# First two w_mod pieces on four column tiles, sums of x first, six accumulators by turns, modulation batches moved ahead of their units

## Chip, cores and metric

One core of one Trainium2 chip runs the whole program in one launch. The metric is the device time of that launch in microseconds. TensorE is called PE here, VectorE DVE, ScalarE ACT, GpSimd POOL, and SyncE, whose queue issues nearly all loads, SP.

## What is computed

A single layer of a decoder trunk for 256 prompt tokens and 8 sample tokens, which share the weights: 264 columns in all, kept feature-major as 16 blocks of 128 features. Cut to what matters here:

```python
mod = jax.nn.silu(c) @ prm['w_mod'] + prm['b_mod']
shift, scale, gate = jnp.split(mod[:, None, :], 3, axis=-1)
h = rmsnorm(x, prm['g_pre']) * (1 + scale) + shift
(u_a, v_a, z_a, x_b, z_b, q, k, v, q_i, k_i, w_i, z_c, g_m) = split_proj(h @ prm['w_in'])
# three branches (spatial gating, RG-LRU, indexed attention), gated, merged
o = merged @ prm['w_out']
x = x + gate * rmsnorm(o, prm['g_post'])
```

The matrix `w_mod` (2048 by 6144) is multiplied with 9 conditioning vectors only (1 prompt, 8 samples). Nothing that uses `h` can start before shift and scale of at least one block of 128 features are there, and every such block needs its columns of `w_mod` over all 2048 rows.

## The kernel before, in words

All matrix products with 264 columns are done in three fp32r products of split operands: the weight as high part `wh` and rest `wl`, the other side as `hh` and `hl` (`wh*hh + wh*hl + wl*hh`). ACT makes `wh` by a copy (L313), DVE makes `wl` by a subtraction (L317), in halves of 512 columns.

**Pieces of w_mod.** The 16 blocks of `h` are made in six pieces (`PIECES`, L48): block 0, block 1, blocks 2 and 3, 4 to 7, 8 to 11, 12 to 15. A piece's columns of `w_mod` come in loads of 512 KB (4, 4, 8, 16, 16, 16 of them). Here m3.5 is load 5 of piece 3. `mod_item` (L417) holds loads back until `BATCH` of them (1, 2, 2, 4, 4, 4) are there, and then multiplies them (`mod_products`, L405): the stationary side is the conditioning, padded to 32 columns, so that an output takes 32 partitions, and up to four groups of columns of a load go to four column tiles of the array. In pieces 0 and 1 there are two groups of 128 columns, in piece 2 four of 128, in pieces 3 to 5 four of 256. After a piece's last batch `mod_piece` (L467) copies the sums, turns them (`mod_turn`, L446) and makes `hh` and `hl` of its blocks, one step after each product of the units that follow.

**Units.** The weights of the products with 264 columns come in loads of 512 KB, called units here: unit 0 to unit 63 belong to the first 32 output tiles (`EARLY`), which are computed piece by piece of `h`: units 0, 1, 2, 3, 5, 7 of the kernel before hold one block for 8 tiles, units 4 and 6 two blocks for 4 tiles, units 8 to 15 blocks 2 and 3 for 4 tiles each, units 16 to 31 blocks 4 to 7 for 2 tiles each, and so on. Each unit has 24 matmuls, whatever its shape. A tile's partial sum is copied out of PSUM after its first piece (L1042: DVE for even tiles, ACT for odd) and added to by DVE after each further one (L1044). All later products accumulate all 16 blocks in PSUM.

**The order of the work** is the list `STREAM` (L82): `FOLLOW` (L51) says which units go with a piece, and the loop over `units` puts the loads of the next piece between them, spread evenly by `MOD_BY`. Each engine does its instructions in the order of this list. `next_load` (L259) issues loads on SP in the list's order as buffers come free: 6 for units (`raw0` to `raw5`), 8 for w_mod (`rawm0` to `rawm3` and four in `rawx`). A unit's buffer is free when its `wl` is made, a w_mod buffer when PE has multiplied it and the next unit has begun. SP takes its loads strictly in order.

**Accumulators.** PSUM has 8 banks: 3 in the ring `acc`, 3 in the ring `s`, 2 in the ring `t`. Products of the early tiles take `acc`, and every fourth takes `s`, which the turned modulation (`modT`) and the norm's rows (`rsP`, `rbP`) use too.

**The start.** SP loads the conditioning, x in four parts, two loads of piece 0, the first parameters `par`, the other two loads, then units and piece 1. PE runs 40 products of ones first (L186). `norm_x` (L375) sums the squares of x; its first step (the sums, and a product `rsP` on PE) is called after the first load of piece 0 has been multiplied (L1056), the second (`rbP`) after the fourth.

Of the kernel before, what the change touches and what calls it, by code (L numbers as in the profile page):

```python
# [15 lines left out]
P = 128  # L16
# [4 lines left out]
T = NP + NS  # L21
# [25 lines left out]
EARLY = 32  # L47
# [1 line left out]


FOLLOW = [[(0, 0, 1), (8, 0, 1), (16, 0, 1)],  # L51
          [(0, 1, 1), (24, 0, 2), (8, 1, 1), (28, 0, 2), (16, 1, 1)]]
FOLLOW += [[(j, k0, nk) for j in range(0, EARLY, 8 // nk)] for k0, nk in PIECES[2:]]
GATES = [(0, 8), (8, 8)]


NRAW = 6
AHEAD = 2
NEAR = 60
CUT = 2  # L60
MOD_BY = 22

BATCH = [1, 2, 2, 4, 4, 4, 4, 4]

# [14 lines left out]
MODS = _mods()  # L79


def _stream():  # L82


    items, n = [("m", 0, i) for i in range(len(MODS[0]))], 0
    for q, units in enumerate(FOLLOW):
        ms = [("m", q + 1, i) for i in range(len(MODS[q + 1]))] if q + 1 < len(PIECES) else []
        done = 0
        for x, (j, k0, nk) in enumerate(units):
            while done < len(ms) and (x == 2 if q == 0 else done * MOD_BY * len(units) <= x * EARLY * len(ms)):  # L90
                items.append(ms[done])
                done += 1
            items.append(("w", n, [(t, k0, nk) for t in range(j, j + 8 // nk)]))
            n += 1
        assert done == len(ms)
    gate = [("m", q, i) for q in range(len(PIECES), len(MODS)) for i in range(len(MODS[q]))]
    units = 0
    for j in range(EARLY, len(ORDER)):
        for k0 in (0, 8):
            items.append(("w", n, [(j, k0, 8)]))  # L100
            n += 1
            if gate and ORDER[j][0] in ("u", "za", "g0", "pa"):
                if units % 16 in (2, 4, 6, 8):
                    items.append(gate.pop(0))
                units += 1
    assert not gate
    return items
# [33 lines left out]
def trunk_kernel(ctx: ExitStack, tc: tile.TileContext, a: dict, o: dict):  # L141
    nc = tc.nc
    act, dve, pool, pe, sp = nc.scalar, nc.vector, nc.gpsimd, nc.tensor, nc.sync
# [15 lines left out]
    def acc(name):  # L159
        return ps.tile([P, 512], F32, name=name, tag="acc", bufs=3)  # L160

    def pss(name):
        return ps.tile([P, 512], F32, name=name, tag="s", bufs=3)
# [4 lines left out]
    copy = lambda out, x, scale=1.0: act.activation(out, x, AF.Copy, scale=scale)  # L168
# [20 lines left out]
    ident = const.tile([P, P], F32, name="ident")  # L189
# [54 lines left out]
    m0 = len(MODS[0])  # L244
# [10 lines left out]
    resting, units = [], [0]  # L255
# [103 lines left out]
        sp.dma_start(xr[:, 4 * i:4 * i + 4, :], a["xT"][:, 4 * i:4 * i + 4, :])  # L359
    while (i := next_load(0)) is not None:  # L360
        load(i)
        if i == 1:
            sp.dma_start(par[:, 0:C_SH], a["par"][:, 0:C_SH])
    sp.dma_start(par[:, C_SH:C_END], a["par"][:, C_SH:C_END])
    sp.dma_start(pti, bass.AP(tensor=a["pt"].tensor, offset=0, ap=[[0, P], [1, 16]]))
# [9 lines left out]
    def norm_x():  # L375
        add(sqacc, sums[0], sums[1])
        rows = rstd_rows([sqacc])
        next(rows)
        yield
        S["r"] = next(rows)  # L380
        yield
        copy(sqacc, S["r"])
        S["r"] = sqacc

    norm = norm_x()
    pool.tensor_copy(xs, xr[:, :, NP:T])
    dve.tensor_scalar(bsc1, prm(C_BMOD, KB, KB), 1.0, None, op0=OP.add)
    dve.tensor_scalar(hb, prm(C_BA, 0, 2 * KB), 0.5, None, op0=OP.mult)
# [6 lines left out]
    MOD = {}  # L395
# [1 line left out]
    done_h = set()  # L397


    def groups_of(q):  # L400
        width = MODS[q][0][0]
        groups = min(4, width // P)
        return groups, width // groups

    def mod_products(q, m, r):  # L405
        width, ks, _ = MODS[q][m]
        groups, n = groups_of(q)
        if m == 0:
            MOD[q] = pst("pmod")
        for x, k in enumerate(ks):  # L410
            for g in range(groups):
                c = x * width + g * n
                pe.matmul(MOD[q][32 * g:32 * g + 32, 0:n], cpad[:, k, :], r[:, c:c + n],  # L413
                          start=k == 0, stop=k == KB - 1, skip_group_check=True)


    def mod_item(i):  # L417
# [7 lines left out]
        if m == len(MODS[q]) - 1:  # L425
# [17 lines left out]
            else:  # L443
                tasks.spawn(mod_gate(q - len(PIECES)), 1)

    def mod_turn(q, ms):  # L446
        groups, n = groups_of(q)
        r = 32 * groups
        pt = pss("modT")
        for b in range(n // P):  # L450
            pe.transpose(pt[:, b * P:b * P + r], ms[0:r, b * P:(b + 1) * P], ident[0:r, 0:r])
        return pt[:, 0:n].rearrange("p (b g r) -> p b g r", b=n // P, g=4)

    def mod_rows(q):
        groups, n = groups_of(q)
        ms = w("ms")
        copy(ms[0:32 * groups, 0:n], MOD.pop(q)[0:32 * groups, 0:n])
        return ms

    def by_k(x, g):  # L460
# [6 lines left out]
    def mod_piece(q):  # L467
        k0, nk = PIECES[q]
        ms = mod_rows(q)
        yield 1  # L470
        pt = mod_turn(q, ms)
        ks = slice(k0, k0 + nk)
        g = groups_of(q)[0] // 2
        add(by_k(mB[:, ks, :], g), pt[:, :, 0:g, 0:9], by_k1(prm(C_BMOD, k0, nk), g))
        add(by_k(mA[:, ks, :], g), pt[:, :, g:2 * g, 0:9], by_k1(bsc1[:, ks], g))
        mul(mA[:, ks, :], mA[:, ks, :], prm(C_GPRE, k0, nk)[:, :, None].to_broadcast([P, nk, 9]))
        r = S["r"]
        ts, samples = {}, w("hsm")[:, 0:nk * NS].rearrange("p (k b) -> p k b", k=nk)
        for k in range(k0, k0 + nk + 1):
            if k < k0 + nk:  # L480
                t = ts[k] = w("h_")
                stt(t[:, 0:NP], xr[:, k, 0:NP], mA[:, k, 0:1], r[:, 0:NP], OP.mult, OP.mult)
                act.activation(hh[:, k, 0:NP], t[:, 0:NP], AF.Identity, bias=mB[:, k, 0:1])
                if k == k0:
                    mul(samples, xr[:, ks, NP:T], mA[:, ks, 1:9])
                    mul(samples, samples, r[:, None, NP:T].to_broadcast([P, nk, NS]))
                    add(samples, samples, mB[:, ks, 1:9])
                    copy(hh[:, ks, NP:T], samples)
            if k > k0:
                stt(hl[:, k - 1, 0:NP], ts[k - 1][:, 0:NP], mB[:, k - 1, 0:1], f32(hh[:, k - 1, 0:NP]), OP.add,  # L490
                    OP.subtract)
                if k == k0 + 1:
                    sub(hl[:, ks, NP:T], samples, f32(hh[:, ks, NP:T]))
                done_h.add(k - 1)
            yield 1
# [524 lines left out]
    ACC = {}  # L1020

    def product(j, k0, nk, wh, wl):
        kind, f = ORDER[j]
        if k0 == 0 and (kind, f) in BEFORE:
            BEFORE[kind, f]()
        early = j < EARLY
        last = k0 + nk == KB
        if early or k0 == 0:
            ACC[j] = pss("acc") if early and not last and j % 4 == 3 else acc("acc")
        c = ACC[j]  # L1030
        xh, xl = {None: (hh, hl), "a": (S.get("ah"), S.get("al")), "m": (S.get("mh"), S.get("ml"))}[RHS.get(kind)]
        assert RHS.get(kind) or done_h.issuperset(range(k0, k0 + nk))
        for kk in range(nk):
            k = k0 + kk
            for n, (x, y) in enumerate(((wh, xh), (wh, xl), (wl, xh))):
                pe.matmul(c[:, 0:T], x[:, kk * P:(kk + 1) * P], y[:, k, :],  # L1036
                          start=n == 0 and (kk == 0 if early else k == 0),
                          stop=n == 2 and (kk == nk - 1 if early else k == KB - 1))
        if early:
            pj = part[j // KB][:, j % KB, :]  # L1040
            if k0 == 0:
                (copy if j % 2 else dve.tensor_copy)(pj, c[:, 0:T])  # L1042
            elif not last:
                add(pj, c[:, 0:T], pj)  # L1044
            else:
                x = w("sum")
                add(x, c[:, 0:T], pj)
                tasks.spawn(POST[kind](f, x), 1)
        elif last:
            tasks.spawn(POST[kind](f, c[:, 0:T]), 1)  # L1050
        tasks.run()

    for i, it in enumerate(items):
        while (x := next_load(units[0])) is not None:
            load(x)
        if i == 1:  # L1056
            next(norm)
        late = it[0] == 'w' and ORDER[it[2][0][0]][0] == "zb"
        pieces = len(it[2]) if it[0] == "w" else 0
        if i >= m0 and not late:  # L1060
            split_plan()
            split_some(CUT // 2 if pieces > 2 else None)
        if it[0] == "m":
            mod_item(i)
            continue
        units[0] += 1
        wh, wl = SPLIT.pop(i)
        col = 0
        for j, k0, nk in it[2]:
            product(j, k0, nk, wh[:, col:col + nk * P], wl[:, col:col + nk * P])  # L1070
            col += nk * P
            if col == 4 * P:
                split_some()
        if late:
            split_plan(AHEAD - 1)
            split_some()
# [16 lines left out]
    p = pss("rsP")  # L1093
# [120 lines left out]
```

## Time and profile before

| | |
|---|---|
| median of 3 runs | 1578.3 us (1578.22 to 1578.94) |
| the profiled execution: its own time | 1578.65 us |
| its span on the core | 1577.0 us |
| PE busy | 1555.5 us (99%), 13353 matmul records |
| DVE busy | 982.5 us (62%) |
| ACT busy | 806.8 us (51%) |
| DMA | 326.26 MB, mean 207 GB/s |

A view lists times in microseconds from the span's start. "Idle before, releaser" is how long the engine stood idle just before an instruction, and whose instruction ended the wait. The helpers copy, mul, add, sub and stt stand under their own lines (L168 to L172). A matmul with fp32 operands shows as two records. PE's records overlap, since a matmul is pipelined: its pace is read from the distance of the starts, not from the durations. PEclk is the clock that PE was granted, 1.00 for 2.4 GHz and 0.50 for 1.2 GHz. For a DMA the profile gives the start of its issue on SP and the time from there until the data had landed.

### The profile page before, as it was taken

Reading aid. Unit: us, or ns where it says so; the run is one execution under the profiler, and the core shown is the slowest. Engines: PE = TensorE matmul, PEld = TensorE weight load, DVE = VectorE, ACT = ScalarE, POOL = GpSimd, SP = SyncE. Lnnn points to the kernel's source line nnn. Section 1 sums busy time; section 2 is a strip of 40 time slices with the busy share of each in tenths; the row PEclk is TensorE's granted clock in tenths of the full one; section 3 lists DMA queues with packets and bytes.
Section 4 is the critical chain, followed back from the end, with each engine's and each line's share of the span. In section 5 each row is a group of like instructions: output and inputs, shape, how many; then the busy total and the mean of one; then the engine's idle time right before and its main releaser. Section 6 shows DMA issues by size and latency. Waiting matters only on the chain.

```text
span 1577.0 us, 33367 instructions
## 1 busy us (share of the span) xinstructions
PE 1555.5 (99%) x13353; PEld 1516.0 (96%) x13353; DVE 982.5 (62%) x2097; ACT 806.8 (51%) x1628; POOL 133.7 (8%) x240
## 2 busy tenths in 40 slices
PE   8999999999999999999999999999999999999997
PEld 8789898999999999999999999999999999999997
DVE  6777589755567446455556544445777777766554
ACT  5334368555555444444444443344777777744442
POOL 0000027000000001000000000001221111100011
PEclk9999999999999999999999999999999999999999
DMA  9898863646555556556656676665555555555652
GB/s 376 333 353 305 310 199 121 229 160 206 169 176 174 189 185 201 182 180 216 224 190 202 224 277 223 205 205 168 168 173 168 188 180 174 177 183 183 240 177 81
DMA packets 94907, 326.26 MB, mean 207 GB/s; under 512 B 10784, under 2 KB 14240, under 8 KB 94368
## 3 DMA queue, kind: packets, MB, share of 16 engines
q1 hardware_dynamic: 93952, 322.98, 59.7%
q8 instruction: 105, 1.72, 0.4%
q10 hardware_dynamic: 800, 1.15, 0.2%
q14 instruction: 50, 0.41, 0.1%
HBM read 320.35 MB, written 3.67 MB: 205 GB/s over the span
## 4 chain that ended last, share of the span: by engine, by line
PE 83%; DVE 1%; POOL 0%; ACT 0%; issue 0%; DVEq 0%; POOLq 0%; ACTq 0%
PE acc L1036 78%; PE pmod L413 1%; PE spP L864 0%; PE sP L699 0%; PE oP L711 0%; PE giP L905 0%; PE gaP L905 0%; POOL qq L589 0%; PE ssP L748 0%; PE soP L772 0%; PE sP L698 0%; PE pT L706 0%; PE oP L713 0%; PE vaP L665 0%; DVE x L172 0%
## 5 line engine op out<-in xcount | busy, mean ns | idle before, releaser
L171 DVE TENSOR_TENSOR wl<-raw,wh 128x512 fp32r<-128x512 f32 x964 | 636.3, 704 | 368.3 <-ACT wh L168 358.8
L1036 PE MATMUL acc<-hh,wh 128*128 128x264 f32 x2832 | 816.7, 288 | 7.3 <-DVE part L170 3.9
L1036 PE MATMUL acc<-hl,wh 128*128 128x264 f32 x2832 | 804.1, 284 | 0.0
L1036 PE MATMUL acc<-hh,wl 128*128 128x264 f32 x2832 | 802.7, 283 | 1.4 <-DVE wl L171 1.3
L168 ACT ACTIVATE wh<-raw 128x512 fp32r<-128x512 f32 x964 | 551.8, 622 | 487.2 <-PE acc L1036 363.2
L1036 PEld LDWEIGHTS acc<-hh,wh 128*128 128x128 f32 x2832 | 534.1, 189 | 21.7 <-issue 13.0
L1036 PEld LDWEIGHTS acc<-hl,wh 128*128 128x128 f32 x2832 | 534.5, 189 | 0.8 <-DVE hl L171 0.2
L1036 PEld LDWEIGHTS acc<-hh,wl 128*128 128x128 f32 x2832 | 531.8, 188 | 1.9 <-DVE wl L171 1.9
L1036 PE MATMUL acc<-ah,wh 128*128 128x264 f32 x768 | 217.9, 284 | 0.0
L1036 PE MATMUL acc<-al,wh 128*128 128x264 f32 x768 | 217.6, 283 | 0.0
L1036 PE MATMUL acc<-ah,wl 128*128 128x264 f32 x768 | 217.4, 283 | 0.0
L1036 PEld LDWEIGHTS acc<-al,wh 128*128 128x128 f32 x768 | 144.7, 188 | 0.0
L1036 PEld LDWEIGHTS acc<-ah,wh 128*128 128x128 f32 x768 | 144.6, 188 | 0.0
L1036 PEld LDWEIGHTS acc<-ah,wl 128*128 128x128 f32 x768 | 144.0, 187 | 0.0
L170 DVE TENSOR_TENSOR part<-acc,part 128x264 f32<-128x264 f32 x120 | 48.7, 428 | 38.9 <-PE acc L1036 38.7
L1036 PE MATMUL acc<-mh,wh 128*128 128x264 f32 x256 | 72.6, 284 | 0.0
L1036 PE MATMUL acc<-ml,wh 128*128 128x264 f32 x256 | 72.5, 283 | 0.0
L1036 PE MATMUL acc<-mh,wl 128*128 128x264 f32 x256 | 72.5, 283 | 0.0
L836 POOL TENSOR_TENSOR mg<-mg,gp 128x264 f32<-128x264 f32 x16 | 12.0, 753 | 465.2 <-DVE gp L172 465.2
L1036 PEld LDWEIGHTS acc<-ml,wh 128*128 128x128 f32 x256 | 48.2, 188 | 0.0
L1036 PEld LDWEIGHTS acc<-mh,wh 128*128 128x128 f32 x256 | 48.2, 188 | 0.0
L1036 PEld LDWEIGHTS acc<-mh,wl 128*128 128x128 f32 x256 | 48.0, 187 | 0.0
(375 smaller groups left out, 1075.5 us busy)
## 6 DMA issues: line engine op xcount, KB each, us to landing
raw<-in_wall SPq DMA_DIRECT2D x482, 512.0 KB, 3.6
rawm<-in_wmod SPq DMA_DIRECT2D x64, 512.0 KB, 7.2
rawx<-in_wmod SPq DMA_DIRECT2D x32, 512.0 KB, 8.9
gkv<-in_ckv SPq DMA_DIRECT2D x32, 256.0 KB, 4.5
xr<-in_xT SPq DMA_DIRECT2D x4, 528.0 KB, 5.3
wrg<-in_wrg SPq DMA_DIRECT2D x1, 2048.0 KB, 12.8
x<-in_xp SPq DMA_DIRECT2D x1, 2048.0 KB, 8.1
out_yp<-x SPq DMA_DIRECT2D x8, 256.0 KB, 3.1
```

The costliest lines, as they stand in the source:

```text
L168: copy = lambda out, x, scale=1.0: act.activation(out, x, AF.Copy, scale=scale)
L170: add = lambda out, x, y: dve.tensor_tensor(out, x, y, OP.add)
L171: sub = lambda out, x, y: dve.tensor_tensor(out, x, y, OP.subtract)
L413: pe.matmul(MOD[q][32 * g:32 * g + 32, 0:n], cpad[:, k, :], r[:, c:c + n], start=k == 0, stop=k == KB - 1, skip_group_check=True)
L836: pool.tensor_tensor(S["mg"][:, j, :], S["mg"][:, j, :], x, OP.add)
L1036: pe.matmul(c[:, 0:T], x[:, kk * P:(kk + 1) * P], y[:, k, :], start=n == 0 and (kk == 0 if early else k == 0), stop=n == 2 and (kk == nk - ...
```

## The change

Pieces 0 and 1 use four column tiles of 64 columns instead of two of 128, and their sums are turned by two small products with a rearranged identity. The sums of x (`rsP`) come before piece 0, and `par` is loaded after all four loads of piece 0. Early products go to the rings `acc` and `s` by turns (six banks). Copies out of PSUM in units of two blocks are all done by ACT. In `FOLLOW` the units of two blocks for new tiles go one place later (the old units 4 and 5, and 6 and 7, change places). Instead of the even spread, `VISITS` says ahead of which unit of a piece each batch of the next piece stands: for pieces 3, 4 and 5 the first batch stands ahead of the previous piece's first unit, the others after 1, 3 and 5 units (piece 3) or 3, 6 and 9 (pieces 4 and 5). In piece 3 the making of `h` has one more step between a block's `h` and the `hl` of the block before it.

```diff
 FOLLOW = [[(0, 0, 1), (8, 0, 1), (16, 0, 1)],
-          [(0, 1, 1), (24, 0, 2), (8, 1, 1), (28, 0, 2), (16, 1, 1)]]
+          [(0, 1, 1), (8, 1, 1), (24, 0, 2), (16, 1, 1), (28, 0, 2)]]
...
+VISITS = [(2, 2), (0, 1, 3, 4), (0, 1, 3, 5), (0, 3, 6, 9), (0, 3, 6, 9)]
...
-            while done < len(ms) and (x == 2 if q == 0 else done * MOD_BY * len(units) <= x * EARLY * len(ms)):
+            while done < len(ms) and x >= VISITS[q][done // BATCH[q + 1]]:
...
-        if i == 1:
+        if i == m0 - 1:
             sp.dma_start(par[:, 0:C_SH], a["par"][:, 0:C_SH])
...
     norm = norm_x()
+    next(norm)
...
-    def groups_of(q):
-        width = MODS[q][0][0]
-        groups = min(4, width // P)
-        return groups, width // groups
+    def group_of(q):
+        return MODS[q][0][0] // 4
...
-            for g in range(groups):
+            for g in range(4):
                 c = x * width + g * n
                 pe.matmul(MOD[q][32 * g:32 * g + 32, 0:n], cpad[:, k, :], r[:, c:c + n],
                           start=k == 0, stop=k == KB - 1, skip_group_check=True)
...
     def mod_turn(q, ms):
-        groups, n = groups_of(q)
-        r = 32 * groups
+        n = group_of(q)
         pt = pss("modT")
+        if n < P:
+            rows = ident.rearrange("p (a g r) -> p g a r", a=2, g=2)
+            for g in range(2):
+                pe.matmul(pt[n * g:n * g + n, 0:64], ms[:, 0:n], rows[:, g], start=True, stop=True,
+                          skip_group_check=True)
+            return pt[:, 0:64].rearrange("p (b g r) -> p b g r", b=1, g=2)
...
                     copy(hh[:, ks, NP:T], samples)
+            if nk == 4 and q == 3 and k > k0:
+                yield 1
...
-            ACC[j] = pss("acc") if early and not last and j % 4 == 3 else acc("acc")
+            ACC[j] = pss("acc") if early and not last and j % 2 else acc("acc")
...
-                (copy if j % 2 else dve.tensor_copy)(pj, c[:, 0:T])
+                (copy if j % 2 or nk > 1 else dve.tensor_copy)(pj, c[:, 0:T])
...
-        if i == 1:
-            next(norm)
```

PE's first instructions, before: `pmod` are the products of piece 0, `rsP` the sums of x's squares, `rbP` their spread over the partitions, `modT` the turned sums, `acc` unit 0.

```order
L186 MATMUL warm<-ones 128x128 x40
L413 MATMUL pmod<-rawm_169,cpad 32x128 x8
L344 MATMUL rsP<-ones,sqacc 128x1 x3
L413 MATMUL pmod<-rawm_170,cpad 32x128 x8
L413 MATMUL pmod<-rawm_171,cpad 32x128 x8
L413 MATMUL pmod<-rawm_172,cpad 32x128 x8
L353 MATMUL rbP<-dg,ones 128x264
L451 MATMUL modT<-ident,ms 128x64
L1036 MATMUL acc<-hh,wh 128x264
```

The same place after the change:

```order
L187 MATMUL warm<-ones 128x128 x40
L345 MATMUL rsP<-ones,sqacc 128x1 x3
L413 MATMUL pmod<-rawm_169,cpad 32x64 x16
L413 MATMUL pmod<-rawm_170,cpad 32x64 x16
L413 MATMUL pmod<-rawm_171,cpad 32x64 x16
L413 MATMUL pmod<-rawm_172,cpad 32x64 x16
L354 MATMUL rbP<-dg,ones 128x264
L454 MATMUL modT<-ident,ms 64x64 x2
L1045 MATMUL acc<-hh,wh 128x264
```

The sums of x moved ahead of piece 0, and each load is multiplied by twice as many products of half the columns.

SP's loads that follow m2.4 to m2.7, up to m3.7, before (`raw_167`, `raw_168` and `raw_163` to `raw_166` are the six buffers of units, here units 10 to 15; `rawm` and `rawx` hold w_mod):

```order
L277 DMA raw_167<-in_wall 128x1024
L277 DMA raw_168<-in_wall 128x1024
L275 DMA rawm_169<-in_wmod 128x1024
L275 DMA rawm_170<-in_wmod 128x1024
L277 DMA raw_163<-in_wall 128x1024
L275 DMA rawm_171<-in_wmod 128x1024
L275 DMA rawm_172<-in_wmod 128x1024
L277 DMA raw_164<-in_wall 128x1024
L275 DMA rawx<-in_wmod 128x1024 x2
L277 DMA raw_165<-in_wall 128x1024
L275 DMA rawx<-in_wmod 128x1024 x2
```

The same place after the change:

```order
L278 DMA raw_167<-in_wall 128x1024
L276 DMA rawm_169<-in_wmod 128x1024
L276 DMA rawm_170<-in_wmod 128x1024
L278 DMA raw_168<-in_wall 128x1024
L276 DMA rawm_171<-in_wmod 128x1024
L276 DMA rawm_172<-in_wmod 128x1024
L278 DMA raw_163<-in_wall 128x1024
L278 DMA raw_164<-in_wall 128x1024
L276 DMA rawx<-in_wmod 128x1024 x2
L278 DMA raw_165<-in_wall 128x1024
L276 DMA rawx<-in_wmod 128x1024 x2
```

Two units changed places with loads of w_mod; m3.7, the last of these rows, is the thirteenth load after m2.7 in both.

DVE while piece 3's `h` is made, before (`h__` is a block's scaled x, `hl` its low part, `wl` the low part of a unit's weights, `part` a partial sum):

```order
L172 SCALAR_TENSOR_TENSOR h__1218<-xr_173,mA_124,sqacc_129 128x256
L172 SCALAR_TENSOR_TENSOR hl_248<-h__1203,mB_125,hh_247 128x256
L171 TENSOR_TENSOR hl_248<-hsm_1202,hh_247 128x4x8
L170 TENSOR_TENSOR part1_250<-acc_1223,part1_250 128x264
L172 SCALAR_TENSOR_TENSOR h__1231<-xr_173,mA_124,sqacc_129 128x256
L172 SCALAR_TENSOR_TENSOR hl_248<-h__1218,mB_125,hh_247 128x256
L171 TENSOR_TENSOR wl_1240<-raw5_168,wh_1239 128x512
L170 TENSOR_TENSOR part1_250<-acc_1243,part1_250 128x264
L172 SCALAR_TENSOR_TENSOR h__1251<-xr_173,mA_124,sqacc_129 128x256
L172 SCALAR_TENSOR_TENSOR hl_248<-h__1231,mB_125,hh_247 128x256
L170 TENSOR_TENSOR part1_250<-acc_1255,part1_250 128x264
L172 SCALAR_TENSOR_TENSOR hl_248<-h__1251,mB_125,hh_247 128x256
```

The same place after the change:

```order
L173 SCALAR_TENSOR_TENSOR h__1245<-xr_173,mA_124,sqacc_129 128x256
L171 TENSOR_TENSOR part1_268<-acc_1248,part1_268 128x264
L173 SCALAR_TENSOR_TENSOR hl_266<-h__1230,mB_125,hh_265 128x256
L172 TENSOR_TENSOR hl_266<-hsm_1229,hh_265 128x4x8
L172 TENSOR_TENSOR wl_1263<-raw4_167,wh_1262 128x512
L171 TENSOR_TENSOR part1_268<-acc_1266,part1_268 128x264
L173 SCALAR_TENSOR_TENSOR h__1274<-xr_173,mA_124,sqacc_129 128x256
L171 TENSOR_TENSOR part1_268<-acc_1277,part1_268 128x264
L173 SCALAR_TENSOR_TENSOR hl_266<-h__1245,mB_125,hh_265 128x256
L172 TENSOR_TENSOR wl_1263<-raw4_167,wh_1262 128x512
L171 TENSOR_TENSOR part1_268<-acc_1288,part1_268 128x264
L173 SCALAR_TENSOR_TENSOR h__1296<-xr_173,mA_124,sqacc_129 128x256
```

An addition of a partial sum now stands between any two steps of `h`; the same work runs over units 13 to 15, where it ran over units 14 and 15.

## Rows read from the trace of the kernel before

**Rows 1.** The page: busy time, share of the span, instructions.

```profile
PE 1555.5 (99%) x13353; PEld 1516.0 (96%) x13353; DVE 982.5 (62%) x2097; ACT 806.8 (51%) x1628; POOL 133.7 (8%) x240
```

**Rows 2.** Stretches: PE, PEld, DVE, ACT, POOL busy; PEclk, DMA share, GB/s.

```profile
30.00:40.00 10.00, 8.54 (x86) 7.72 (x83) 6.92 (x22) 4.39 (x12) 0.00 (x0) 1.00 1.02 412
...
50.00:60.00 10.00, 7.97 (x89) 6.98 (x81) 7.42 (x23) 4.27 (x11) 0.00 (x0) 1.00 0.94 349
...
120.00:140.00 20.00, 20.00 (x196) 17.86 (x196) 11.73 (x27) 5.84 (x11) 0.00 (x0) 1.00 0.94 358
```

**Rows 3.** What PE waited for, 18 to 96 us: total, times, longest.

```profile
PE acc L1036 <- DVE part L170: 3.9, 3, 1.6
...
PE acc L1036 <- ACT wh L168: 1.1, 1, 1.1
...
PE pmod L413 <- DMA rawm<-in_wmod: 0.2, 1, 0.2
```

**Rows 4.** PE in order of time: start, length, what, idle before; units 9 to 16.

```profile
63.13 0.28 PE L1036 MATMUL acc<-hh,wh 128*128 128x264 f32 x1
...
65.93 0.28 PE L1036 MATMUL acc<-hh,wl 128*128 128x264 f32 x1
66.14 1.93 PE L413 MATMUL pmod<-rawm,cpad 128*32 128x256 f32 x32
68.01 0.39 PE L1036 MATMUL acc<-hh,wh 128*128 128x264 f32 x1
...
94.30 0.36 PE L1036 MATMUL acc<-hh,wh 128*128 128x264 f32 x1 [1.61 <-DVE part L170]
```

**Rows 5.** SP in order of time: issues of m2.4 to m2.7, and of m3.6 and m3.7.

```profile
32.14 4.12 SPq L275 DMA_DIRECT2D rawx<-in_wmod  x4
...
56.03 0.86 SPq L275 DMA_DIRECT2D rawx<-in_wmod  x2
```

**Rows 6.** DMA issued 35.9 to 36.2 us (m2.7): KB, us to landing.

```profile
rawx<-in_wmod SPq DMA_DIRECT2D x1, 512.0 KB, 10.2
```

**Rows 7.** DMA issued 56.5 to 56.6 us (m3.7).

```profile
rawx<-in_wmod SPq DMA_DIRECT2D x1, 512.0 KB, 6.7
```

**Rows 8.** DMA issued 24.7 to 25.0 us (m2.1).

```profile
rawm<-in_wmod SPq DMA_DIRECT2D x1, 512.0 KB, 9.8
```

**Rows 9.** PE in order of time: the start, piece 1, a batch of piece 2.

```profile
14.58 2.81 PE L413 MATMUL pmod<-rawm,cpad 128*32 128x128 f32 x48
...
20.01 0.45 PE L1036 MATMUL acc<-hh,wh 128*128 128x264 f32 x1 [1.77 <-ACT hh L168]
...
28.48 3.69 PE L413 MATMUL pmod<-rawx,cpad 128*32 128x128 f32 x64
...
38.84 0.39 PE L1036 MATMUL acc<-hh,wh 128*128 128x264 f32 x1 [1.22 <-DVE part L170]
...
40.49 1.08 PE L413 MATMUL pmod<-rawm,cpad 128*32 128x128 f32 x32
```

**Rows 10.** DVE in order of time: a unit's `wl`, its additions, a step of `h`.

```profile
85.78 1.28 DVE L171 TENSOR_TENSOR wl<-raw,wh 128x512 fp32r<-128x512 f32 x2
...
89.41 0.19 DVE L169 TENSOR_TENSOR hsm<-xr,mA 128x32 f32<-128x32 f32 x1
...
90.31 0.47 DVE L172 SCALAR_TENSOR_TENSOR h__1218<-xr,mA,sqacc 128x256 f32<-128x256 f32 x1
```

**Rows 11.** Stretches, PE alone: PE busy, PEclk, DMA share, GB/s.

```profile
17.00:20.00 3.00, 1.24 (x11) 1.00 1.03 412
20.00:21.00 1.00, 0.99 (x2) 0.60 1.01 401
...
23.00:24.00 1.00, 1.00 (x8) 0.69 1.05 418
56.00:60.00 4.00, 1.97 (x13) 1.00 0.98 365
```

**Rows 12.** The page's costliest groups: xcount | busy us, mean ns | idle before.

```profile
L170 DVE TENSOR_TENSOR part<-acc,part 128x264 f32<-128x264 f32 x120 | 48.7, 428 | 38.9 <-PE acc L1036 38.7
```

More of the change, by code (lines that the diff above doesn't have):

```diff
@@ L60 @@
 CUT = 2
-MOD_BY = 22
 BATCH = [1, 2, 2, 4, 4, 4, 4, 4]
@@ L446, in mod_turn @@
     def mod_turn(q, ms):
-        groups, n = groups_of(q)
-        r = 32 * groups
+        n = group_of(q)
         pt = pss("modT")
+        if n < P:
[4 more added lines that the diff above has]
+            return pt[:, 0:64].rearrange("p (b g r) -> p b g r", b=1, g=2)
         for b in range(n // P):
-            pe.transpose(pt[:, b * P:b * P + r], ms[0:r, b * P:(b + 1) * P], ident[0:r, 0:r])
+            pe.transpose(pt[:, b * P:b * P + P], ms[:, b * P:(b + 1) * P], ident)
         return pt[:, 0:n].rearrange("p (b g r) -> p b g r", b=n // P, g=4)
     def mod_rows(q):
-        groups, n = groups_of(q)
+        n = group_of(q)
         ms = w("ms")
-        copy(ms[0:32 * groups, 0:n], MOD.pop(q)[0:32 * groups, 0:n])
+        copy(ms[:, 0:n], MOD.pop(q)[:, 0:n])
         return ms
@@ L472, in mod_piece @@
         ks = slice(k0, k0 + nk)
-        g = groups_of(q)[0] // 2
+        g = pt.shape[2] // 2
         add(by_k(mB[:, ks, :], g), pt[:, :, 0:g, 0:9], by_k1(prm(C_BMOD, k0, nk), g))
```

## Prediction

> **What bounds the kernel now.** I read the page first: PE is busy 99% of the span and DVE 62% [rows 1], so time can only come out of stretches in which PE stands still, runs at half clock, or does products that the change makes cheaper. Next the stretches: from 100 us on PE is busy without a break, 20.00 of 20.00 us at 120 to 140 [rows 2], and nothing there is touched. Ahead of 100 us it is not: 8.54 and 7.97 of 10 us in two of the slices, with the DMA share at or near 1 [rows 2]. The list of waits gives these holes a name: PE waits for DVE's additions (3.9 us in 3 waits, the longest 1.6) and for `wh` (1.1), and hardly for a load (0.2) [rows 3]. So PE seems to be held up by DVE and ACT, and the change goes at just these waits. But in the same stretch the loads come at 412 GB/s without a hole, and the DMA queue thins out only near 60 us (share 0.94) [rows 2]. What PE can do sooner is therefore limited by when its data are there. The view that decides is that of the loads: when SP issues them and how long they take to land [rows 5 to 8].
>
> **The term that decides.** I follow one load, m3.7. In the changed order the second batch of piece 3 (m3.4 to m3.7) stands ahead of unit 9; before, it stood behind unit 10. When can m3.7 be there? m2.7 was issued at 35.9 (the end of the row of four that starts at 32.14 and lasts 4.12, less its own issue) and landed 10.2 us later, at 46.1 [rows 5, 6]. m3.7 is the thirteenth load after it in both orders. At 412 GB/s [rows 2] a load of 512 KB (0.524 MB) takes 1.27 us, so the thirteenth is there at 46.1 + 16.6 = 62.7 at the earliest. Before, it landed at 56.5 + 6.7 = 63.2 [rows 5, 7], since SP had waited now and then for a buffer. I take 62.7: buffers come free sooner in the new order, and with some 10 us of loads in the queue [rows 6, 8] an issue that is late by 1 us leaves no hole.
>
> Will PE be there by then? A step from matmul to matmul in a unit is 0.12 us and a unit has 24, which makes 2.92 (63.13 to 65.93 and one step [rows 4]). A batch of four loads in pieces 3 to 5 costs 68.01 - 65.93 - 0.12 = 1.96 us [rows 4], one of two loads in piece 2 about 1.1 [rows 9]. In the trace of before unit 3 ends ahead of the batch at 40.49, with a wait of 1.22 in it [rows 9], so unit 2 ended near 36. With no gain at the start PE then does m2.0 and m2.1 (the second landed at 24.8 + 9.8 = 34.6 [rows 8] at the latest), units 3 to 8, the other three batches of piece 2 and the first of piece 3: 36 + 1.1 + 6 x 2.92 + 3 x 1.1 + 1.96 = 59.9. So PE stands before m3.4 at 59.9 or sooner, and the last load of that batch comes at 62.7. A quarter of 1.96 and a semaphore later **unit 9 starts, at 63.3**; before, it started at 63.13 [rows 4].
>
> **The sum.** From unit 9's start to unit 16's the trace of before has 94.30 - 63.13 = 31.17 us [rows 4]: seven units, four batches (m3.0 to m3.15), one turn, and two waits, 1.61 [rows 4] and 0.23 (the 0.2 in [rows 3]). The new order has the same units and the turn, but three batches: m3.0 to m3.7 are done, and m4.0 to m4.3 are added. The waits go: the 1.61 us was a wait for a free accumulator while DVE made piece 3's `h`; that work now begins a unit sooner, has the batch m4.0 to m4.3 ahead of unit 16 as cover, and six banks instead of mostly three. That makes 31.17 - 1.96 - 1.84 = 27.37, and unit 16 starts at 90.7. In the old order it started at 94.30 with m4.0 to m4.3 still to do, which is as good as 96.26. The gain is 5.6 us: two batches of 1.96 done while PE would have waited, 1.84 of waits, less 0.2 for the later start of unit 9. I keep 0.5 us back for waits of some tenths on DVE that the new order may have, and take **5.1 us**.
>
> Would it be lost later? The loads m4.0 to m4.3 can be issued when m3.8 to m3.11 are multiplied, some 18 us ahead of unit 16, against 10.2 us of queue at the fullest [rows 6]. From there on PE is the slowest (DMA share 0.94 at 120 to 140 with PE busy throughout [rows 2]), and the end moves with it.
>
> **What the other parts bring: nothing of their own, as long as m3.7 decides.**
> - Four tiles of 64 columns. Piece 1 takes 3.69 us for 64 records of 128 columns on two tiles; 32 records on four tiles take 1.08 with 128 columns [rows 9] and 1.93 with 256 [rows 4]. If columns are what is paid, piece 1 takes 1.85; if each record on four tiles keeps its price, 128 x 1.08 / 32 = 4.3, a loss of 0.6. I take 1.85, since the price nearly doubles from 128 to 256 columns. Piece 0 likewise: its last 48 records take 2.81 [rows 9], half of it would bring unit 0 from 20.01 to 18.6.
> - x's sums first. Their three products change places with those of the first load, and the chain behind them on DVE runs while piece 0 is multiplied. The load of `par` moves behind two others; what needs it (`bsc`) moved behind that chain on DVE. A gain or loss of some tenths, in the 1.4 us of the line above.
> - Both together bring PE to m2.1 up to 3.2 us sooner, where it waits until 34.6, and to m3.4 near 58. DMA is the cover; without it they would be worth up to 3.2 us. I book 0.
> - Six accumulators and ACT's copies take away the waits ahead of 60 us (2.3 of the 3.9 us, the 1.1 for `wh` [rows 3]). They lie ahead of unit 9 too and are covered.
> - The turn by two small products: a few tenths in pieces 0 and 1, covered.
> - DVE in units 13 to 15: 12 additions at 0.41 [rows 12], four halves of `wl` at 0.64, eight steps of 0.47 and seven small ones of 0.19 [rows 10], 12.6 us, against 3 x 2.92 + 1.96 = 10.7 for PE up to unit 16. The last `hl` comes ahead of two additions and a half of `wl`, at about 11.1, and unit 16 wants it with its eleventh matmul, at 11.9. Bounds 0 and 1.6, as before; I take 0, with the 0.5 above.
>
> **The rivals.**
> 1. *Half clock.* While PE waits for m3.4 to m3.7 it does 2 us of work in 4 to 5 us. In 17 to 20 us PE was busy 1.24 of 3 us, and the clock then stood at half from about 20.2 to 23.6 (mean 0.60 in the first slice, 0.69 in the last); after 56 to 60, with 1.97 of 4 us busy, it stayed at 1.00 [rows 11]. The new stretch lies close to the second case, towards the first. Half clock for as long as then costs up to 1.7 us, of which part falls into the wait; I put it at 0.7 to 1.5: a gain of 4.0, 1574.3. The Trainium skill ("TensorE: Matmul & The Clock Gate", section "HAM oscillation") says that waits for DMA between bursts of matmuls bring the array back to its low clock; by that rule this rival would be the likelier case. The trace bears it out at 20 us and not at 58, and I stay with the full clock by a little.
> 2. *DMA is not the limit.* If m3.7 came when PE wants it, all early gains would count: 3.2 us, and the 5.2 of waits [rows 3]: 8.4, 1569.9. Against it: a DMA share of 1.02 [rows 2].
> 3. *Waits come back behind unit 9.* DVE late by 1.6 us at unit 16, as before, and m3.11 or m3.15, which by the pace of 1.27 are there only 0 to 1.5 us ahead of PE, late by 1: a gain of 2.5, 1575.8.
> 4. *Slower: the four tiles don't run side by side.* If 64 columns cost a full product (3.69 / 32 = 0.115) and the tiles went one after the other, pieces 0 and 1 would take 14.7 us each instead of 3.7: 22 us more ahead of unit 2. DMA covers 2.8 of it (59.9 to 62.7) and 5.1 are gained, so from 8 us on it decides; at 22 the time is 1592. Against it: 32 records in 1.08 us on four tiles [rows 9].
>
> **How the numbers follow.** The sum is made against the profiled execution, 1578.65, which lies 0.35 above the median of 1578.3; from the median, 1578.3 - 5.1 = 1573.2. Chances: forecast (a gain of 4.5 to 6.1) 0.55, half clock 0.22, no limit by DMA 0.06, waits again 0.12, slower 0.05. The range leaves out rival 4 and most of rival 2: from 1571.4 (m3.7 a good 1 us sooner, nothing held back) to 1576.0 (rival 3). A measurement of this kernel can tell some 0.2%, 3.2 us, from no change: faster takes in the forecast, half clock and rival 2, 0.83; rival 3 lies within, 0.12; slower 0.05.
>
> **What would show it.** PE's waits for additions and `wh` ahead of 60 us are nearly gone; in their place `pmod` waits for loads, 4 to 7 us in all, up to 2.5 ahead of unit 3 and most in the batch m3.4 to m3.7. That batch ends near 63, unit 16 starts near 91, and the DMA share is 1 up to 65 us. Piece 1 takes about 1.9 us and unit 0 starts near 18.6. I am wrong if unit 9 starts ahead of 61 or after 65, if the clock is at half after 60, if PE waits for `part` at unit 16, or if the end moves by more or less than unit 16.

## The result, and the profile after

The changed kernel takes **1570.53 us** (median of 6 runs, 1569.29 to 1571.05), the kernel before 1578.26 (6 runs, 1577.79 to 1578.97): a ratio of 0.9949, 95% interval 0.9938 to 0.9959, 7.73 us faster. The forecast was 1573.2 with a range from 1571.4: the direction is right, the gain is 2.6 us larger than forecast, and the time lies 0.9 us below the range. The profiled execution took 1569.65 us, its span is 1567.9.

PE's row of the page, to be held against [rows 1]:

```profile
PE 1549.3 (99%) x13487; PEld 1512.3 (96%) x13487; DVE 981.3 (63%) x2093; ACT 808.2 (52%) x1632; POOL 131.8 (8%) x240
```

What PE waited for from 18 to 96 us (total, times, longest), to be held against [rows 3]:

```profile
PE pmod L413 <- DMA rawx<-in_wmod: 2.2, 2, 1.6
PE acc L1045 <- ACT hh L169: 1.8, 1, 1.8
PE pmod L413 <- DMA rawm<-in_wmod: 1.0, 2, 0.6
```

The waits for additions (3.9) and for `wh` (1.1) are gone, and 3.2 us of waits for loads of w_mod stand in their place. The stretches (PE, PEld, DVE, ACT, POOL busy; PEclk, DMA share, GB/s) show the loads without a hole up to 70 us, where the DMA share had been 0.94 at 50 to 60 [rows 2]:

```profile
20.00:30.00 10.00, 9.94 (x175) 9.50 (x175) 6.40 (x14) 5.83 (x14) 0.00 (x0) 0.76 1.01 390
...
50.00:60.00 10.00, 10.00 (x129) 8.07 (x123) 7.91 (x23) 5.50 (x14) 0.00 (x0) 1.00 1.02 407
60.00:70.00 10.00, 7.75 (x79) 6.37 (x75) 5.13 (x12) 1.79 (x4) 0.00 (x0) 1.00 1.02 406
```

PE in order of time: the batch m3.4 to m3.7, then the first matmuls of units 9, 16, 54 and 63:

```profile
59.19 1.07 PE L413 MATMUL pmod<-rawx,cpad 128*32 128x256 f32 x16
61.87 0.64 PE L413 MATMUL pmod<-rawx,cpad 128*32 128x256 f32 x8 [1.61 <-DMA rawx<-in_wmod]
63.15 0.64 PE L413 MATMUL pmod<-rawx,cpad 128*32 128x256 f32 x8 [0.64 <-DMA rawx<-in_wmod]
63.72 0.39 PE L1045 MATMUL acc<-hh,wh 128*128 128x264 f32 x1
...
90.59 0.39 PE L1045 MATMUL acc<-hh,wh 128*128 128x264 f32 x1
...
218.54 0.28 PE L1045 MATMUL acc<-hh,wh 128*128 128x264 f32 x1
...
259.93 0.37 PE L1045 MATMUL acc<-hh,wh 128*128 128x264 f32 x1
```

The same two late marks in the kernel before, and ahead of them the seam between units 30 and 31 (the place where one unit's last matmul meets the next unit's first):

```profile
146.75 0.28 PE L1036 MATMUL acc<-hl,wh 128*128 128x264 f32 x1
146.87 0.28 PE L1036 MATMUL acc<-hh,wl 128*128 128x264 f32 x1
147.10 0.36 PE L1036 MATMUL acc<-hh,wh 128*128 128x264 f32 x1
...
225.61 0.28 PE L1036 MATMUL acc<-hh,wh 128*128 128x264 f32 x1
...
268.38 0.37 PE L1036 MATMUL acc<-hh,wh 128*128 128x264 f32 x1
```

Unit 9 starts at 63.72 (forecast 63.3) and unit 16 at 90.59 (forecast 90.7). Before, unit 16 started at 94.30 with one batch of 1.96 more to do [rows 4], so **5.67 us are gained there**: the forecast's sum, without the 0.5 kept back. But the gain goes on growing, though by the forecast nothing behind 100 us is touched. At unit 54 it is 225.61 - 218.54 = 7.07 us, at unit 63 268.38 - 259.93 = 8.45, and the spans differ by 9.1. (The two profiled executions lie 1.3 us further apart than the medians: 0.39 above its median before, 0.88 below it after. From unit 63 to the end the runs here take 1307.6 to 1308.6 us, whatever was changed, so the last 0.65 of the 9.1 lie within that scatter.) So 1.40 us come from units 16 to 54 and 1.38 from units 54 to 63, and neither is in the sum.

In the second stretch lie the eight products of q_i, for each of which POOL copies samples into `qipad` and makes the low part `qq`. PE's waits there, before, and after:

```profile
PE lgP L595 <- POOL qq L589: 1.4, 3, 0.5
```

```profile
PE ssP L634 <- ACT srelu L631: 0.8, 1, 0.8
PE lgP L604 <- POOL qq L598: 0.3, 1, 0.3
```

POOL in order of time, the first and the last step of that chain, before, and after:

```profile
223.67 0.67 POOL L582 COPY qipad<-sum 64x4 f32<-64x4 f32 x4 [10.86 <-DVE sum L170]
...
247.19 1.86 POOL L589 TENSOR_TENSOR qq<-sum,qq 64x256 fp32r<-64x256 f32 x2
```

```profile
215.63 1.13 POOL L591 COPY qipad<-sum 64x4 f32<-64x4 f32 x4 [8.58 <-DVE sum L171]
...
238.22 1.54 POOL L598 TENSOR_TENSOR qq<-sum,qq 64x256 fp32r<-64x256 f32 x2
```

Before, the chain takes 247.19 + 1.86 - 223.67 = 25.4 us, 3.17 a product, where a unit of PE takes 2.92; it begins 1.94 us ahead of unit 54. After, it begins 2.91 ahead of unit 54 and takes 24.1.

### The profile page after: what moved, and what is told of

The parts are those of the page before. It is cut to its first block, busy times and chain, and to the rows that moved or that the text cites. A ratio compares the mean times of both kernels' runs of the same rounds, so it can differ in the third digit from the quotient of the medians.

```text
span 1567.9 us, 33624 instructions
## 1 busy us (share of the span) xinstructions
PE 1549.3 (99%) x13487; PEld 1512.3 (96%) x13487; DVE 981.3 (63%) x2093; ACT 808.2 (52%) x1632; POOL 131.8 (8%) x240
## 4 chain that ended last, share of the span: by engine, by line
PE 94%; DMA 3%; DVE 2%; issue 1%; ACT 1%; SPq 0%; DVEq 0%; ACTq 0%
PE acc L1045 87%; PE pmod L413 2%; DMA rawm<-in_wmod 2%; DMA rawx<-in_wmod 1%; PE spP L873 0%; PE sP L708 0%; PE oP L720 0%; PE giP L914 0%; PE gaP L914 0%; DVE wl L172 0%; PE ssP L757 0%; PE soP L781 0%; PE sP L707 0%; PE pT L715 0%; PE oP L722 0%
```

## The experiments

Theory A is the forecast's: what counts is the batches done while PE would have waited, and loads set the pace up to unit 9. Theory B: the start and the accumulators carry the gain. Theory C, formed on the result: in the q_i products POOL's chain holds PE, and whatever lets it start sooner or shortens it gains there. All kernels compute the whole layer. Each ratio is to the kernel before, with its 95% interval. The kernel before, run beside each group of experiments, had medians of 1578.32 to 1578.74; the changed kernel was not run beside them, so that a difference of times between an experiment and the changed kernel is uncertain by some half a microsecond, and the starts of units in the traces say more.

**The new places of the batches alone.**

```diff
-          [(0, 1, 1), (24, 0, 2), (8, 1, 1), (28, 0, 2), (16, 1, 1)]]
+          [(0, 1, 1), (8, 1, 1), (24, 0, 2), (16, 1, 1), (28, 0, 2)]]
+VISITS = [(2, 2), (0, 1, 3, 4), (0, 1, 3, 5), (0, 3, 6, 9), (0, 3, 6, 9)]
...
-            while done < len(ms) and (x == 2 if q == 0 else done * MOD_BY * len(units) <= x * EARLY * len(ms)):
+            while done < len(ms) and x >= VISITS[q][done // BATCH[q + 1]]:
```

> The kernel before with the new places of the batches alone (VISITS and FOLLOW; no four tiles of 64, no early sums, no six accumulators, no extra step in h). Theory A (the gain is batches done while PE would have waited; m3.7 sets the pace): unit 9 starts at 63.2 to 63.8, unit 16 at 90.6 to 92.3, since the wait for an accumulator there (1.6 us before) may come back; a gain of 4 to 5.7, 1572.6 to 1574.3 us. Theory B (the start and the accumulators carry the gain, the order only shifts work): a gain of at most 2 us, 1576.3 or more.

Measured: 1573.08 us (1572.28 to 1573.48), ratio 0.9961 [0.9948, 0.9975], 5.5 us faster. Unit 9 starts at 63.96, unit 16 at 93.72. PE's waits, 18 to 96 us:

```profile
PE acc L1036 <- DVE part L170: 1.9, 2, 1.5
PE acc L1036 <- ACT hh L168: 1.8, 1, 1.8
```

Theory B falls: two thirds of the gain need neither the new start nor the accumulators. The 1.5 us wait for an accumulator came back, as was allowed for, but unit 16 is 1.4 us beyond the bound of 92.3: from unit 14 to unit 16 this run takes 10.68 us, the changed kernel 7.83, and the list of waits shows 1.9 of the 2.85 between them. (A wait is counted from the end of the record ahead of it: what shows as 1.54 us is a step of 1.83 between starts instead of 0.12.) Units 54 to 63 take 41.04 us, where they took 42.77 before, so the gain in the q_i products comes with the order.

**The accumulators and ACT's copies alone.**

```diff
-            ACC[j] = pss("acc") if early and not last and j % 4 == 3 else acc("acc")
+            ACC[j] = pss("acc") if early and not last and j % 2 else acc("acc")
-                (copy if j % 2 else dve.tensor_copy)(pj, c[:, 0:T])
+                (copy if j % 2 or nk > 1 else dve.tensor_copy)(pj, c[:, 0:T])
```

> The kernel before with the six accumulators and ACT's copies alone. Theory A: PE's waits for additions and wh ahead of 60 us (2.3 and 1.1) go, and the waits of 0.1 to 0.2 us at the seams of units 30 to 53 go too (1.4 us in all between units 16 and 54), but loads take the place of the first: unit 16 starts 1 to 3 us sooner, 1574 to 1577 us. Theory B: 5 us or more sooner, 1573.3 or less.

Measured: 1575.53 us (1574.0 to 1576.65), ratio 0.9979 [0.9970, 0.9989], 3.0 us faster. Unit 16 starts at 90.13, 4.17 us sooner and not 1 to 3. Then PE meets the next late thing, the low part of `h`, a little further on:

```profile
92.63 0.39 PE L1036 MATMUL acc<-hl,wh 128*128 128x264 f32 x1 [1.50 <-DVE hl L172]
```

Of the 4.17 us, 1.8 are given back within units 16 and 17. Units 54 to 63 take 42.74 us, as before. The gains of this run and the last, 3.0 and 5.5, come to 8.5 where the change has 7.7: they hardly overlap.

**POOL's copies into `qipad` halved in number, in the kernel before.**

```diff
-            for s in range(2):
-                pool.tensor_copy(qipad[64 * e:64 * e + 64, :, 48 * s + 2 * j + e],
-                                 qs[64 * e:64 * e + 64, :, s])
+            pool.tensor_copy(qipad[64 * e:64 * e + 64, :, 2 * j + e:2 * j + e + 49:48], qs[64 * e:64 * e + 64])
```

> The kernel before with POOL's four copies into qipad for each product of q_i done as two (same bytes). Theory C (ahead of 250 us POOL's chain of eight steps, 25.4 us, is slower than PE's eight units, 23.4, and PE waits for it): a step falls from 3.17 to about 2.6 us, below PE's 2.92, the three waits for qq (1.4 us) go and 1.4 to 2.2 us are gained: 1576.0 to 1576.9. Rival (DVE, busy 10.00 of 10 us at 240 to 250, holds PE as soon as POOL does not): within 0.5 of before, 1577.8 or more.

Measured: 1576.25 us (1575.19 to 1578.47), ratio 0.9986 [0.9977, 0.9995], 2.3 us faster. POOL, first and last step of the chain:

```profile
221.99 0.43 POOL L581 COPY qipad<-sum 64x8 f32<-64x8 f32 x2 [10.29 <-DVE sum L170]
...
243.11 1.62 POOL L587 TENSOR_TENSOR qq<-sum,qq 64x256 fp32r<-64x256 f32 x2
```

The chain takes 22.7 us (2.84 a product, below PE's 2.92; the 2.6 expected was too low), and units 54 to 63 take 41.18 instead of 42.77. Theory C holds: in the kernel before, POOL's chain costs 1.6 us. (Unit 16 starts at 93.19 here, 1.1 us sooner than in the kernel before, though the edit touches nothing ahead of it: two executions with the same work can differ by as much there. From unit 16 to 54 they differ by far less, 131.12 us here and 131.31 before.)

**The start as before, in the changed kernel.**

```diff
-        if i == m0 - 1:
+        if i == 1:
             sp.dma_start(par[:, 0:C_SH], a["par"][:, 0:C_SH])
...
     norm = norm_x()
-    next(norm)
...
-    def group_of(q):
-        return MODS[q][0][0] // 4
+    def groups_of(q):
+        width = MODS[q][0][0]
+        groups = min(4, width // P)
+        return groups, width // groups
...
+        if i == 1:
+            next(norm)
```

`mod_products`, `mod_turn` and `mod_rows` are those of the kernel before, too.

> The changed kernel with the start as before: two tiles of 128 columns in pieces 0 and 1, x's sums after the first load of piece 0, par after two loads. Theory A: loads cover it; unit 9 starts at 63.5 to 64.0 and PE waits some 2 us less for loads ahead of it; the time is within 0.7 of the changed kernel's, 1569.9 to 1571.3. Theory B: the 1.9 us of each of the pieces 0 and 1 are on the path: 1573 or more.

Measured: 1569.47 us (1568.37 to 1570.65), ratio 0.9943 [0.9929, 0.9956]: nothing lost, as theory A wants, 0.4 us below what was expected and 1.1 us less than the changed kernel's median, with ranges that overlap. PE's waits for loads of w_mod from 18 to 96 us fall from 3.2 to 1.1 us:

```profile
PE pmod L414 <- DMA rawx<-in_wmod: 1.1, 2, 0.6
```

Unit 9 starts at 62.78, ahead of what was expected, because the loads came earlier: m3.7 lands at 62.16 and in the changed kernel at 63.10. `par` takes 0.33 us of the stream in either place. Of the 0.94 us, 0.2 come from a hole between two loads near 17 us (0.5 us instead of 0.7), 0.3 from a load near 24 us that takes 1.57 in the changed kernel where its neighbours take 1.28, and 0.35 from the load of page numbers (1.23 instead of 1.58). Why these vary is open.

**Without the extra step in piece 3's `h`.**

```diff
-            if nk == 4 and q == 3 and k > k0:
-                yield 1
```

> The changed kernel without the extra step in piece 3's h. Theory A: hl is complete sooner, but additions stand behind two steps of h; unit 16 starts within 0.5 us of the changed kernel's 90.6, and the time is within 0.7 of it, 1569.9 to 1571.3 us. Rival (the step is what keeps PE from waiting for additions at unit 16): 1.0 to 1.6 us slower.

Measured: 1570.11 us (1569.96 to 1571.98), ratio 0.9950 [0.9937, 0.9964]. Unit 16 starts at 91.12, 0.53 later, since from unit 9 to 16 it takes 27.61 us instead of 26.87. By unit 63 nothing is left of it (259.96 and 259.93), and it doesn't show in the time.

**POOL's copies halved, in the changed kernel** (the same edit as above).

> The changed kernel with POOL's copies into qipad halved in number. Theory C (the new order already lets POOL's chain begin early enough, PE waits 0.3 us for it): units 54 to 63 take 40.9 to 41.4 us as in the changed kernel (41.4), a gain of 0 to 0.5, 1570.0 to 1570.5 us. Rival (POOL still sets the pace there): a gain of 1.5 us or more, 1569.0 or less.

Measured: 1570.54 us (1569.16 to 1570.96), ratio 0.9949 [0.9936, 0.9963], at the edge of what was expected; units 54 to 63 take 41.19, where they take 41.39 in the changed kernel. The order and the shorter chain each reach about 41.1, and both together no less: it is one and the same wait that they remove.

**Piece 3's batches later.**

```diff
-VISITS = [(2, 2), (0, 1, 3, 4), (0, 1, 3, 5), (0, 3, 6, 9), (0, 3, 6, 9)]
+VISITS = [(2, 2), (0, 1, 3, 4), (0, 2, 4, 5), (0, 3, 6, 9), (0, 3, 6, 9)]
```

> The changed kernel with piece 3's batches ahead of units 8, 10, 12 and 13 instead of 8, 9, 11 and 13. Theory A (PE stands before m3.4 to m3.7 until they land): PE does unit 9 in that time, the two waits there (1.6 and 0.6 us) go, unit 10 starts at 63.6 to 64.2 instead of 66.7, and unit 16 at 87.6 to 89.1 instead of 90.6, the next bound being m3.15 (75.9): a gain of 1.5 to 3 us, 1567.5 to 1569.0. Rival (loads that free their buffers later, or DVE at unit 16, take it back): within 0.5.

Measured: 1567.81 us (1567.40 to 1567.84), ratio 0.9930 [0.9917, 0.9944], 2.7 us below the changed kernel, and no run of the two overlaps. PE in order of time, the batch m3.4 to m3.7 (now behind unit 9, which starts at 59.35), units 10 and 16:

```profile
62.38 1.93 PE L413 MATMUL pmod<-rawx,cpad 128*32 128x256 f32 x32
...
64.24 0.39 PE L1045 MATMUL acc<-hh,wh 128*128 128x264 f32 x1
...
88.70 0.39 PE L1045 MATMUL acc<-hh,wh 128*128 128x264 f32 x1
```

The batch runs in one piece, without a wait. (At unit 63 the gain is 1.7.)

**The two small loads of the start later.**

```diff
-    sp.dma_start(par[:, C_SH:C_END], a["par"][:, C_SH:C_END])
-    sp.dma_start(pti, bass.AP(tensor=a["pt"].tensor, offset=0, ap=[[0, P], [1, 16]]))
...
+        if i == 60:
+            sp.dma_start(par[:, C_SH:C_END], a["par"][:, C_SH:C_END])
+            sp.dma_start(pti, bass.AP(tensor=a["pt"].tensor, offset=0, ap=[[0, P], [1, 16]]))
```

> The changed kernel with the two small loads at the start (the second part of par, and the page table) behind unit 16's time instead of ahead of unit 6's load; they hold the stream of loads for 0.6 and 1.6 us near 30 us. Theory A (the stream of loads sets the time up to unit 9): all later loads land up to 2.2 us sooner, m3.7 at 60.9 to 62.4, unit 9 at 61.6 to 63.1, unit 16 at 88.4 to 90.0; a gain of 0.6 to 2.2 us, 1568.3 to 1569.9. Rival (PE or DVE sets it): unit 16 at 90.3 to 90.8, no gain.

Measured: 1567.29 us (1567.11 to 1567.51), ratio 0.9928 [0.9914, 0.9942], 3.2 us below the changed kernel. PE's batch m3.4 to m3.7 and unit 9:

```profile
57.71 1.07 PE L411 MATMUL pmod<-rawx,cpad 128*32 128x256 f32 x16
59.67 0.64 PE L411 MATMUL pmod<-rawx,cpad 128*32 128x256 f32 x8 [0.89 <-DMA rawx<-in_wmod]
61.03 0.64 PE L411 MATMUL pmod<-rawx,cpad 128*32 128x256 f32 x8 [0.73 <-DMA rawx<-in_wmod]
61.60 0.39 PE L1043 MATMUL acc<-hh,wh 128*128 128x264 f32 x1
```

m3.7 lands at 60.99, 2.11 us sooner, unit 9 starts 2.12 sooner, and nothing was changed but when loads land. That settles that loads set the pace up to unit 9. (At unit 63 the gain is 2.4; the rest of the 3.2 is the 0.9 by which the changed kernel's profiled execution lies below its median.)

**The accumulators and copies as before, in the changed kernel** (the second edit, backwards).

> The changed kernel with the accumulators and the copies out of PSUM as before (three banks and every fourth in the other ring; even tiles by DVE). Theory A with the seams (six banks remove the 1.6 us wait at unit 16, which the sum had, and waits of some tenths at the seams of units 16 to 54, which it had not): unit 16 at 92.0 to 93.7, units 16 to 54 0.5 to 1.4 us longer than the changed kernel's 127.95, units 54 to 63 unchanged at 41.0 to 41.5; 1572.3 to 1573.9 us. Rival (the order alone brings all of it): within 0.7 of 1570.5.

Measured: 1571.94 us (1571.47 to 1572.95), ratio 0.9961 [0.9948, 0.9975], 1.4 us slower than the changed kernel, a little less than expected. Unit 16 starts at 91.92, 0.1 ahead of the bounds, and waits for additions are back ahead of it:

```profile
85.88 0.39 PE L1045 MATMUL acc<-hh,wh 128*128 128x264 f32 x1 [0.29 <-DVE part L171]
88.41 0.39 PE L1045 MATMUL acc<-hh,wh 128*128 128x264 f32 x1 [0.80 <-DVE part L171]
...
220.61 0.28 PE L1045 MATMUL acc<-hh,wh 128*128 128x264 f32 x1
```

From unit 9 to 16 it takes 28.52 us, 1.65 more than the changed kernel. Units 16 to 54 take 220.61 - 91.92 = 128.69 us. The run with the new order alone gives the same, 128.69; the changed kernel takes 127.95, and the kernel before 131.31, less the batch of 1.96, 129.35. So of the 1.40 us, **0.74 is the accumulators'** and 0.66 the order's.

**All three later edits together, with the new start and with the old.**

> The changed kernel with piece 3's batches ahead of units 8, 10, 12 and 13, the two small loads later, and POOL's copies halved. Theory A: the two gains overlap, since both remove the same waits for loads; unit 16 at 86.5 to 88.0, 1565.0 to 1566.7 us, faster than either alone (1567.8, 1567.3). Rival (DVE's additions and h hold unit 16 once loads do not): no better than 1567.3.

> The same as e10, with the start of the kernel before (two tiles of 128 columns, x's sums second, par after two loads). Theory A (the start's gain is covered as long as loads set the pace, and counts when they don't): 0.3 to 2 us behind e10. Rival (the start brings nothing even then, as its longer half clock gives it back): within 0.3 of e10.

Measured: **1565.27 us** (1565.05 to 1566.02), ratio 0.9918 [0.9904, 0.9931], with the new start, the fastest of all; 1567.24 us (1566.62 to 1567.59), ratio 0.9929 [0.9915, 0.9942], with the old. With the new start unit 9 begins at 57.69 and unit 16 at 86.55, with the old at 59.95 and 88.81. What PE still waits for from 18 to 96 us, new start:

```profile
PE acc L1041 <- ACT hh L169: 1.8, 1, 1.8
PE acc L1041 <- DVE part L1047: 1.6, 1, 1.6
```

No wait for a load is left, and now the new start counts, with 2.0 us: it was covered by the loads, as the forecast had it, and is worth something as soon as the cover goes.

## Why the prediction was wrong, and where it was right

- **The term that decides** was right. m3.7 landed at 63.10 (forecast 62.7) and unit 9 started at 63.72 (63.3); moving only loads moved unit 9 by as much. PE came to the batch at 59.19 (forecast: 59.9 or sooner). PE's waits for loads were 3.2 us from 18 us on, where 4 to 7 were forecast.
- **The sum** came out right to 0.1 us at unit 16 (90.59 for 90.7), but by luck: unit 9 came 0.4 late, and units 9 to 16 took 26.87 instead of 27.37. Two terms that the sum takes off were too small. By the distance of PE's starts the two waits cost 1.77 and 0.40 us, not 1.61 and 0.23 (from 92.41 to 94.30 the step is 1.89 instead of 0.12), and a batch costs 2.06, not 1.96, since the step from the first matmul behind it to the next takes 0.23 instead of 0.12. The 0.5 kept back for small waits was not needed. Two executions with the same work also differ by more than 0.1 at unit 16.
- **The step that failed** is "nothing there is touched" and "the end moves with it": behind unit 16 the sum has 0, and 1.40 + 1.38 us came out there. That the end moves by more than unit 16 was among the forecast's own signs of being wrong. The forecast took a busy share of 100% for proof that no time can come out behind 100 us. The kernel before shows, in its stretch from 95 to 225 us,

```profile
95.00:225.00 130.00, 129.97 (x1180) 120.01 (x1179) 88.41 (x194) 52.91 (x102) 1.36 (x6) 1.00 0.82 291
```

  and yet units 16 to 54 lost 1.40 us there. PE's records overlap: from 146.87 to 147.10 the step is 0.23 instead of 0.12, and the record of 0.28 covers it. Most such steps of 0.2 and more follow a batch, but those at 146.87, 149.98, 202.20 and 205.36 follow an ordinary matmul, at the ends of units 30, 31, 46 and 47, where DVE makes pieces 4's and 5's `h`; after the change they are gone. With the slower step behind each (0.20), these four cost 0.86 us. Every run here with three banks in `acc` and every fourth product in `s` has four such seams, whatever the order, and none with six banks has them: that is what the accumulators bring behind unit 16, less 0.15 of new small steps in unit 16. Of the rest, 0.39 are two late products `vP` in the kernel before (at 218.16 and 221.97), for which PE waits for ACT's `vt`, and 0.1 belongs to the batch, which costs 2.06 and was taken at 1.96. What shows all of these is the distance of the starts, not the busy time.
- **Units 54 to 63** were not looked at, though the waits of PE named POOL there (1.4 us). The change gains 1.38 us there, net of a new wait of 0.8 for ACT, and the order alone 1.73, net of the same. That POOL's chain is what held PE is shown by shortening it. Why it starts 1.0 us sooner against PE in the new order is only argued: DVE has done piece 5's last `hl` at 191.8, 7.2 us ahead of unit 48, where before it was done at 203.9, 1.8 ahead of it, so that DVE and ACT enter these products with a lead.
- "What the other parts bring: nothing of their own, as long as m3.7 decides" held for the start: undoing it lost nothing, and it counts for 2.0 us only once the loads no longer cover it. For the accumulators it was too little: without them PE takes 1.65 us more from unit 9 to 16, which is most of the waits that the sum takes away, and 0.74 more behind unit 16.
- Rival 1, half clock, did not come. Between 59 and 63.7 us PE waited 1.61 and 0.64 us, and the granted clock stayed at 1.00, the level of 2.4 GHz. The Trainium skill ("TensorE: Matmul & The Clock Gate", section "HAM oscillation") tells of waits for DMA between bursts, longer than these, that bring the low clock back; these two, with a batch's products on either side, didn't. Ahead of unit 0, where PE waited 1.78 us for ACT, the clock did fall to half (0.50 from 18 to 24 us). Over the start it was lower than before (0.90 at 10 to 20 and 0.76 at 20 to 30, where before it was 1.00 and 0.83); behind it PE still waited 3.2 us for loads, which cover that too.
- Rival 2 gives 1569.9, near the measured time, but for a reason that the runs exclude: loads did set the pace.
- Rivals 3 and 4 did not come: the list of PE's waits has none for an addition at unit 16, and piece 1 takes 2 us on its four tiles.

## What to carry to other kernels

When a forecast says that an early gain is handed on unchanged, look behind it for the places where another engine is just in time or a little late, which neither a full busy share nor the list of waits rules out: steps between starts that are longer than usual, and chains on a slow engine that run at nearly PE's pace. Whatever gives that engine a lead gains again at each of them. And where a stream of loads decides, first look at what small transfers stand in it, then at which product could be put in front of the load that is late.

## What the runs showed of the hardware

- The load of 16 page numbers, spread to 128 partitions (8 KB), held the stream of loads: in the changed kernel the part of `par` ahead of it landed at 29.51 us, it at 31.09 and the next 512 KB at 32.40, where such loads follow each other every 1.28. In the runs whose loads were followed it took 1.23 to 1.66. So 8 KB cost about as much as 512 KB. Its row in the kernel before, by the view of DMA (KB, us to landing):

```profile
pti<-in_pt SPq DMA_DIRECT2D x1, 8.0 KB, 9.9
```
- A batch costs what its columns cost: piece 1's 128 records of 64 columns on four tiles took 1.99 us, as 32 records of 256 columns take 1.93 [rows 4], and 64 records of 128 on two tiles 3.69 [rows 9].

```profile
27.72 1.99 PE L413 MATMUL pmod<-rawx,cpad 128*32 128x64 f32 x128
```
- DVE's steps on `score` (128 by 128 and 128 by 256) that run beside POOL's chain took from 0.34 to over 1 us each in the kernel before, with a mean of 0.57 over both shapes. The lengths go with which of POOL's steps lies beside. The seven of 128 by 256 beside copies into `qipad` alone took 0.47 each, and the five beside the subtraction `qq`, which reads two tiles, 1.01 to 1.03. Of 128 by 128, the seven beside `qq` took 0.40 to 0.87, and the other eight 0.34. In the changed kernel, though, four steps of 128 by 256 share about half of their length with `qq` and take 0.47 to 0.48, so that lying beside is not all. The Trainium skill ("GPSIMD Engine Reference", section "1. Specifications") says that POOL shares its SBUF interfaces with DVE, with contention where a DVE instruction has two SBUF inputs; these steps have such inputs, and the rows beside `qq` agree, those beside the copies show no such cost.

```profile
L172 DVE SCALAR_TENSOR_TENSOR score<-relu,wn,score 128x128 f32<-128x128 f32 (+1 forms) x30 | 15.2, 565 | 0.6 <-ACT relu L599 0.6
```
- The changed kernel's runs spread over 1.8 us, those of the two kernels with later batches or later small loads over 0.4 each. What varies is open.
